# Output projection of a two-layer hybrid trunk: post-norm weight and residual on VectorE in place, and the next layer's first turns pinned behind tiles 3 and 5

## The chip, the cores and the metric

The kernel runs on one core of a Trainium2 chip. The metric is device time in microseconds (us) of one execution. Engines are named as in the profile: PE is TensorE's matmul queue (PEld its weight loads), DVE is VectorE, ACT is ScalarE, POOL is GpSimd, and SP is SyncE, which here only issues DMAs.

## The reference

Two layers, each over 1024 rows of 1024 features. What the change touches is the end of a layer and the start of the next one: the output product, the post-norm with its weight `post_g`, the residual, and the next layer's pre-norm.

```python
def rms_norm(x, g):
    xf = x.astype(jnp.float32)
    y = xf * lax.rsqrt(jnp.mean(xf * xf, axis=-1, keepdims=True) + EPS)
    return (y * g.astype(jnp.float32)).astype(x.dtype)

def hybrid_layer(x, positions, pre_g, w_in, ..., branch_g, w_out, post_g):
    h = rms_norm(x, pre_g)
    proj = h @ w_in
...
    y = jnp.concatenate([
        rms_norm(ya, branch_g[:LRU_WIDTH]),
        rms_norm(yb, branch_g[LRU_WIDTH:LRU_WIDTH + MLA_WIDTH]),
        rms_norm(yc, branch_g[LRU_WIDTH + MLA_WIDTH:]),
    ], axis=-1)
    return x + rms_norm(y @ w_out, post_g)
```

## The kernel before

All arithmetic is fp32; a product is made of three matmuls of split operands (`mm3`, L124 to L126). A layer ends with the output projection (loop from L1084), over eight tiles `t` of 128 rows.

For each tile, `project(t, 0, 5)` splits five of the eight k-slices of the branch outputs Y into high and low parts (ACT L356, POOL L357), runs 30 matmuls into one PSUM tile (pw_63) and moves the result to the SBUF tile `z` with the row scale `ra` (ACT L1001). `project(t, 5, 8)` does the same for the other three slices with 18 matmuls into pw_64, and DVE L1003 adds its result, scaled by `rb`, to `z`. So a tile is 48 matmuls, and its pw_63 must have been read by L1001 before the next tile's first part may write there. Tiles 0 and 1 have their first part made early, inside the attention stage.

Then the post-norm and the residual: POOL L1096 writes `zg = z * g` into a third buffer; `row_rsqrt` forms the row's factor `r` (a sum of squares on ACT L318, then two small POOL instructions, L132 and L133); DVE L1100 makes `z = zg * r + x` in one instruction; SP stores it (L1101). In layer 0 the next layer's pre-norm follows: the same ACT L318, POOL L132 and L133, and DVE L329, which writes the normalised tile into the buffer that held `x` (tiles 0 to 3) or into free halves of Y (tiles 4 to 7). After tiles 1 and 3, `turn_pair` transposes a pair of normalised tiles on PE (16 turns of 128x128, L340, into the four PSUM tiles pa_65 to pa_68) and splits them (ACT L346, DVE L347) into the next layer's left operand. From tile 4 on the next layer's first weights W are loaded (SP L366) and split (ACT L375; the low part on POOL or DVE, L376). The last tile is handled in column pieces of 512, 256 and 256.

Buffers `z`, `zg`, `x` and the loaded W come from one pool of seven tiles of 128x1024 (F_134 to F_140; F_140 holds the post-norm weight here); R tiles hold the split operands. Within an engine instructions run in a fixed order that a list scheduler chose when the program was built; `keep` (used by the change) pins a chain of instructions to the order in which the code is written. Whatever waits at the head of an engine's queue holds all that stands behind it.

Of the kernel before, what the change touches and what calls it, by code (L numbers as in the profile page):

```python
# [12 lines left out]
ALU = mybir.AluOpType  # L13
# [4 lines left out]
NT = T // 128  # L18
DEPTH = 2
# [68 lines left out]
def trunk_kernel(tc, A, out):  # L88
    nc = tc.nc
    keep = tc.keep_in_program_order  # L90
    V, S_, G, PE = nc.vector, nc.scalar, nc.gpsimd, nc.tensor
# [20 lines left out]
    def bank(kind):  # L112
        turn[kind] = (turn[kind] + 1) % len(banks[kind])
        return banks[kind][turn[kind]]
# [4 lines left out]
    def SM(n):  # L119
        ring_at[0] = (ring_at[0] + 1) % 48  # L120
        return ring[:, ring_at[0], 0:n]

    def mm3(ps, sh, sl, mh, ml, start, stop):
        PE.matmul(ps, lhsT=sh, rhs=mh, start=start, stop=False)  # L124
        PE.matmul(ps, lhsT=sh, rhs=ml, start=False, stop=False)  # L125
        PE.matmul(ps, lhsT=sl, rhs=mh, start=False, stop=stop)  # L126

    def rsqrt(ms, n, out=None):

        y = SM(n) if out is None else out  # L130
        x = SM(n)
        G.tensor_scalar(out=x, in0=ms, scalar1=EPS, scalar2=None, op0=ALU.add)  # L132
        G.tensor_tensor(out=y, in0=x, in1=mhalf[:, 0:n], op=ALU.pow)  # L133
        return y

    identr = cst.tile([128, 128], F32R, name="ident")
    ident = identr.bitcast(F32)
# [25 lines left out]
    FS = Slots(cst, NF, 1024, F32, "F")  # L163
# [10 lines left out]
    def load_x(src, t):  # L174
        x = FS.take((128, 2, 512))
        nc.sync.dma_start(out=x, in_=src[t * 128:(t + 1) * 128, :].rearrange("p (a b) -> p a b", b=512))
        return x
# [133 lines left out]
    def row_rsqrt(xs, cols=((0, 1024),), order=lambda i: i):  # L311

        n = len(xs) * len(cols)
        ms = SM(n)
        for i in range(n):
            q = HS.take((128, 512))
            c = slice(*cols[i // len(xs)])
            order(S_.activation(q.bitcast(BF16)[:, c], xs[i % len(xs)].rearrange("p a b -> p (a b)")[:, c],  # L318
                                AF.Square, scale=1.0 / 32, accum_out=ms[:, i:i + 1]))
            HS.give(q)  # L320
        if len(cols) > 1:
            V.scalar_tensor_tensor(out=ms[:, 0:1], in0=ms[:, 0:1], scalar=ms[:, 1:2], in1=ms[:, 2:3], op0=ALU.add,
                                   op1=ALU.add)
        return rsqrt(ms[:, 0:len(xs)], len(xs))

    def prenorm(xs, ns, order=lambda i: i, eng=None):
        r = row_rsqrt(xs, order=order)
        for i, (x, n) in enumerate(zip(xs, ns)):
            (eng or V).tensor_scalar(out=n, in0=x, scalar1=r[:, i:i + 1], scalar2=None, op0=ALU.mult)  # L329
        return ns  # L330

    def turn_pair(l, xn, hT, pair, slots):

        half, o = pair // 2, (pair % 2) * 256
        for kk in range(4):
            ps = bank("P1")
            pv = ps.rearrange("p (k t) -> p k t", k=2)
            for j in range(2):
                for i in range(2):
                    PE.transpose(pv[:, j, i * 128:(i + 1) * 128],  # L340
                                 xn[i][:, kk // 2, (2 * (kk % 2) + j) * 128:(2 * (kk % 2) + j + 1) * 128], ident)
            h, lo = hT[half][kk]
            for j in range(2):
                hs = h[:, j, o:o + 256]
                g = pg[:, l * 8 + 2 * kk + j:l * 8 + 2 * kk + j + 1]
                S_.activation(hs, pv[:, j], AF.Copy, scale=g)  # L346
                V.scalar_tensor_tensor(out=lo[:, j, o:o + 256], in0=pv[:, j], scalar=g, in1=hs.bitcast(F32),  # L347
                                       op0=ALU.mult, op1=ALU.subtract)
        for x in xn:
            slots.give(x)  # L350

    def new_hT():
        return [(RS.take((128, 2, 512)), RS.take((128, 2, 512))) for _ in range(4)]

    def split(src, h, lo, eng=None):
        S_.activation(h, src, AF.Copy)  # L356
        (eng or G).tensor_tensor(out=lo, in0=src, in1=h.bitcast(F32), op=ALU.subtract)  # L357
# [175 lines left out]
    xn = [load_x(A["x"][0], t) for t in range(2)]  # L533
    ws = {0: W(0, 0, 256, 4)}
    xn += [load_x(A["x"][0], t) for t in range(2, 4)]
    hT = [new_hT()]
    x4 = [load_x(A["x"][0], t) for t in range(4, NT)]
    ws[1] = W(0, 256, 256, 4, now=False)
    prow = load_params()
    prenorm(xn[:2], xn[:2])  # L540
    turn_pair(0, xn[:2], hT, 0, FS)
    prenorm(xn[2:], xn[2:])
    for p in range(2):
        prenorm(x4[2 * p:2 * p + 2], x4[2 * p:2 * p + 2], keep, G)
    turn_pair(0, xn[2:], hT, 1, FS)
    ws[1].split(keep)
    turn_params(prow)
    xn, xs = x4, FS

    for l in range(DEPTH):  # L550

        xc, last, gw = {}, [], []
# [31 lines left out]
        for p in range(2):  # L584
            turn_pair(l, xn[2 * p:2 * p + 2], hT, 2 + p, xs)
# [115 lines left out]
        for t in range(NT):  # L701
            if t % 4 == 0:
# [5 lines left out]
                                   op0=ALU.add, op1=ALU.mult)  # L708
# [52 lines left out]
        for t in range(NT):  # L761
            if t % 2 == 0:
# [8 lines left out]
                            in1=CK[:, t:t + 1].to_broadcast([128, 2, 16]), op=ALU.mult)  # L771
            V.scalar_tensor_tensor(out=r2[:, 1, 0:16], in0=kr[:, 16:32], scalar=-1.0, in1=SK[:, t], op0=ALU.mult,
                                   op1=ALU.mult)
            V.tensor_tensor(out=r2[:, 1, 16:32], in0=kr[:, 0:16], in1=SK[:, t], op=ALU.mult)
            V.tensor_tensor(out=ln[:, 192:256].rearrange("p (a b) -> p a b", a=2),
                            in0=r2[:, 0:1].to_broadcast([128, 2, 32]), in1=r2[:, 1:2].to_broadcast([128, 2, 32]),
                            op=ALU.add)
            r = rsqrt(ms, 2)
# [3 lines left out]
            if t % 4 == 3:  # L782
                half = t // 4
                hs = slice(half * 512, (half + 1) * 512)
                for b in range(3):
# [8 lines left out]
                    for r0, n, h, r1, lo in todo:  # L794
# [3 lines left out]
                                        op=ALU.subtract)  # L798
# [186 lines left out]
        def tile_cols(t):  # L985
            return ((0, 512), (512, 768), (768, 1024)) if t == NT - 1 else ((0, 1024),)

        def project(t, a, b, bufs=None):
            ts = slice(t * 128, (t + 1) * 128)
            yh, yl, z = bufs or (RS.take((128, 8, 128)), RS.take((128, 8, 128)), FS.take((128, 2, 512)))  # L990
            split(Y[:, a:b, ts], yh[:, a:b], yl[:, a:b], G)
            ps = bank("P2")
            zf = z.rearrange("p a b -> p (a b)")
            for c0, c1 in tile_cols(t):
                c = slice(c0, c1)
                for k in range(a, b):
                    for d in range(c0, c1, 512):
                        cs = slice(d, min(d + 512, c1))
                        mm3(ps[:, cs], yh[:, k], yl[:, k], wo[k][0][:, cs], wo[k][1][:, cs], k == a, k == b - 1)
                if a == 0:  # L1000
                    S_.activation(zf[:, c], ps[:, c], AF.Copy, scale=ra[:, t:t + 1])  # L1001
                else:
                    V.scalar_tensor_tensor(out=zf[:, c], in0=ps[:, c], scalar=rb[:, t:t + 1], in1=zf[:, c],  # L1003
                                           op0=ALU.mult, op1=ALU.add)
            return yh, yl, z
# [75 lines left out]
        if l + 1 < DEPTH:  # L1081
            hT = [new_hT()]
        xn = []
        for t in range(NT):  # L1084
            ts = slice(t * 128, (t + 1) * 128)
            xo = load_x(src, t)
            yh, yl, z = started.pop(t, None) or project(t, 0, 5)
            cols = tile_cols(t)
            project(t, 5, 8, (yh, yl, z))
            RS.give(yh)  # L1090
            RS.give(yl)
            zg = FS.take((128, 2, 512))
            zf, zgf, xf, gf = [v.rearrange("p a b -> p (a b)") for v in (z, zg, xo, gpost)]
            for c in cols:
                c = slice(*c)
                G.tensor_tensor(out=zgf[:, c], in0=zf[:, c], in1=gf[:, c], op=ALU.mult)  # L1096
            r = row_rsqrt([z], cols)
            for c in ((0, 512), (512, 1024)) if t == NT - 1 else cols:
                c = slice(*c)
                V.scalar_tensor_tensor(out=zf[:, c], in0=zgf[:, c], scalar=r, in1=xf[:, c], op0=ALU.mult, op1=ALU.add)  # L1100
                nc.sync.dma_start(out=(x1_dram if l == 0 else out[0])[ts, c], in_=zf[:, c])  # L1101
            FS.give(zg)
            if l + 1 < DEPTH:
                if t < 4:
                    xn += prenorm([z], [xo])
                    if t % 2:
                        turn_pair(l + 1, xn, hT, t // 2, FS)
                        xn = []
                else:
                    if t == 4:  # L1110
                        for y in yhalf:
                            YS.lend(y)
                        ws = {0: W(l + 1, 0, 256, 4)}
                        xs = YS
                    n = YS.take((128, 2, 512))
                    xn += prenorm([z], [n])
                    FS.give(xo)
            else:
                FS.give(xo)
            FS.give(z)  # L1120
# [26 lines left out]
```

## Time and profile before

| | before |
|---|---|
| time, median of 3 runs (lowest, highest) | 927.14 us (925.89, 928.77) |
| profiled execution, its own time | 928.23 us |
| its span in the trace | 926.5 us |
| mean granted PE clock, share of full | 0.991 |
| busy: PE, DVE, ACT, POOL | 879.8, 568.7, 520.1, 425.4 us |

The profiled execution is 1.09 us above the median. The output projection of layer 0 lies at about 385 to 475 us of the span, that of layer 1 at about 850 to 926 us. A duration is the time of one instruction; "idle before" is how long its engine had nothing to do until it, and the arrow names what ended that. PE instructions overlap, so for PE the distance from start to start is the pace. Line numbers of rows are those of the kernel before.

### The profile page before, as it was taken

The page shows a single profiled execution, that of the slowest core. Times are in us where ns is not written, and L with a number is a line of the kernel's source. Part 1 is how long each engine was busy: PE and PEld are TensorE (multiplying, and loading weights), DVE is VectorE, ACT ScalarE, POOL GpSimd, SP SyncE. Part 2 cuts the span into 40 slices and gives each one's busy share as a digit, 9 for nine tenths or more (in the row PEclk, how much of TensorE's full clock was granted, in tenths as well). Part 3 has the DMA queues.
Part 4 walks back from the last instruction along what each step waited for, and adds up shares of the span by engine and source line. Part 5 has one row for each costly group of instructions (what it writes and reads, how often), then busy time and mean ns, then how long its engine had stood idle before and what let it go on. Part 6 is the DMA issues. An engine that isn't in the chain of part 4 may idle for free. (4 is left out here: it accounts for less than half of the span.)

```text
span 926.5 us, 13666 instructions
## 1 busy us (share of the span) xinstructions
PE 879.8 (95%) x5078; PEld 778.1 (84%) x5078; DVE 568.7 (61%) x1078; ACT 520.1 (56%) x1032; POOL 425.4 (46%) x461
## 2 busy tenths in 40 slices
PE   4999997999999999989999999989989999999996
PEld 3998786998889889868887888889978999998786
DVE  4567955735689897454456488434554989853322
ACT  6447744554777778444544386354466877754312
POOL 4720056564045567384743000665530567655822
PEclk9999998999999999998999999999999999999999
DMA  7201365322000253022324022753110015221322
GB/s 274 55 25 49 110 226 178 123 100 59 14 1 4 89 182 115 23 91 87 118 93 122 1 80 86 288 201 131 49 23 0 1 47 193 81 69 46 126 102 91
DMA packets 45080, 86.93 MB, mean 94 GB/s; under 512 B 8825, under 2 KB 26837, under 8 KB 45013
## 3 DMA queue, kind: packets, MB, share of 16 engines
q1 hardware_dynamic: 35796, 52.50, 17.8%
q0 software_dynamic: 6912, 25.17, 7.7%
q10 hardware_dynamic: 2304, 8.39, 2.3%
q8 instruction: 40, 0.66, 0.3%
q14 instruction: 28, 0.22, 0.1%
HBM read 60.88 MB, written 25.17 MB: 93 GB/s over the span
## 5 line engine op out<-in xcount | busy, mean ns | idle before, releaser
L124 PE MATMUL pw<-R,R 128*128 128x512 f32 (+1 forms) x704 | 259.7, 370 | 5.1 <-DVE R L357 2.1
L126 PE MATMUL pw<-R,R 128*128 128x512 f32 (+1 forms) x704 | 253.0, 360 | 0.7 <-POOL R L376 0.7
L125 PE MATMUL pw<-R,R 128*128 128x512 f32 (+1 forms) x704 | 253.3, 360 | 0.0
L124 PE MATMUL pa<-R,R 128*128 128x512 f32 (+3 forms) x540 | 187.3, 349 | 11.6 <-DVE F L707 6.6
L125 PE MATMUL pa<-R,R 128*128 128x512 f32 (+3 forms) x540 | 186.1, 345 | 0.0
L126 PE MATMUL pa<-R,R 128*128 128x512 f32 (+3 forms) x540 | 185.2, 345 | 0.0
L124 PEld LDWEIGHTS pw<-R,R 128*128 128x128 f32 x704 | 135.0, 192 | 25.7 <-ACT F L937 2.7
L126 PEld LDWEIGHTS pw<-R,R 128*128 128x128 f32 x704 | 134.9, 192 | 19.1 <-POOL R L376 1.1
L125 PEld LDWEIGHTS pw<-R,R 128*128 128x128 f32 x704 | 135.2, 192 | 17.2
L124 PEld LDWEIGHTS pa<-R,R 128*128 128x128 f32 x540 | 102.0, 189 | 22.5 <-DVE F L707 7.1
L939 POOL TENSOR_SCALAR F<-F,ring 128x128 f32<-128x128 f32 (+3 forms) x96 | 72.7, 762 | 89.5 <-DVE ring L938 87.9
L126 PEld LDWEIGHTS pa<-R,R 128*128 128x128 f32 x540 | 101.8, 189 | 9.9
L125 PEld LDWEIGHTS pa<-R,R 128*128 128x128 f32 x540 | 102.2, 189 | 8.6
L357 DVE TENSOR_TENSOR R<-pa,R 128x512 fp32r<-128x512 f32 (+1 forms) x120 | 73.9, 630 | 16.7 <-ACT R L356 15.7
L937 ACT ACTIVATE F<-pw,ring 128x128 f32<-128x128 f32 (+3 forms) x96 | 71.1, 743 | 21.1 <-DVE ring L935 18.4
L935 DVE TENSOR_REDUCE ring<-pw 128x1 f32<-128x128 f32 (+3 forms) x96 | 71.6, 749 | 11.3 <-PE pw L928 10.7
L356 ACT ACTIVATE R<-pa 128x512 fp32r<-128x512 f32 (+1 forms) x120 | 63.8, 554 | 19.2 <-PE pa L959 17.6
L376 POOL TENSOR_TENSOR R<-F,R 128x1024 fp32r<-128x1024 f32 (+1 forms) x24 | 54.2, 2265 | 42.2 <-ACT R L375 42.2
L968 PE MATMUL pa<-R,R 128*128 128x256 f32 x480 | 72.1, 288 | 0.5 <-DVE R L357 0.5
L968 PEld LDWEIGHTS pa<-R,R 128*128 128x128 f32 x480 | 63.4, 189 | 3.6 <-DVE R L357 1.1
L959 PE MATMUL pa<-ident,F 128*128 128x128 f32 x432 | 63.6, 273 | 0.7 <-DVE H L892 0.4
L357 POOL TENSOR_TENSOR R<-Y,R 128x640 fp32r<-128x640 f32 (+2 forms) x34 | 48.9, 1455 | 27.4 <-ACT R L356 10.2
(300 smaller groups left out, 1360.8 us busy)
## 6 DMA issues: line engine op xcount, KB each, us to landing
F<-in_w_in SPq DMA_DIRECT2D x24, 512.0 KB, 4.7
F<-in_x SPq DMA_DIRECT2D x13, 512.0 KB, 4.7
F<-in_w_out SPq DMA_DIRECT2D x9, 512.0 KB, 3.5
F<-x SPq DMA_DIRECT2D x8, 512.0 KB, 4.5
Y<-in_w_out SPq DMA_DIRECT2D x7, 512.0 KB, 4.4
x<-F SPq DMA_DIRECT2D x7, 512.0 KB
out_y<-F SPq DMA_DIRECT2D x7, 512.0 KB
Y<-in_w_in SPq DMA_DIRECT2D x6, 512.0 KB, 3.6
```

Of the source, the lines that this page charges most:

```text
L124: PE.matmul(ps, lhsT=sh, rhs=mh, start=start, stop=False)
L125: PE.matmul(ps, lhsT=sh, rhs=ml, start=False, stop=False)
L126: PE.matmul(ps, lhsT=sl, rhs=mh, start=False, stop=stop)
L356: S_.activation(h, src, AF.Copy)
L357: (eng or G).tensor_tensor(out=lo, in0=src, in1=h.bitcast(F32), op=ALU.subtract)
L376: self.eng.tensor_tensor(out=lo, in0=st, in1=h.bitcast(F32), op=ALU.subtract)
L935: V.tensor_reduce(out=mx, in_=sv, axis=AX.XY, op=ALU.max, negate=True)
L937: S_.activation(p[:, 0:n].rearrange("p (a b) -> p a b", a=sv.shape[1]), sv, AF.Exp, bias=mx, accum_out=sm)
L939: G.tensor_scalar(out=p[:, 0:n], in0=p[:, 0:n], scalar1=rs, scalar2=1.0, op0=ALU.mult, op1=ALU.mult)
L959: PE.transpose(pv[:, c, i * 128:(i + 1) * 128], p[i][:, b * 128:(b + 1) * 128], ident)
L968: PE.matmul(o, lhsT=sv, rhs=pt[:, part, c * 256:(c + 1) * 256], start=(b == 0 and part == 0), stop=(b == nb - 1 and part == 1))
```

## The change

For tiles 0 to 6 of both layers, POOL L1096 and its buffer `zg` go. DVE does two instructions in place of one, both on `z` itself: `z = z * r * g`, then `z = z + x`. The last tile keeps the old form. `turn_pair` no longer follows tiles 1 and 3: it stands between the two parts of `project` for tile 3 (pair of tiles 0 and 1) and tile 5 (pair of tiles 2 and 3), and its transposes are pinned with `keep`.

```diff
--- before.py
+++ after.py
@@ -329,7 +329,7 @@
             (eng or V).tensor_scalar(out=n, in0=x, scalar1=r[:, i:i + 1], scalar2=None, op0=ALU.mult)
         return ns
 
-    def turn_pair(l, xn, hT, pair, slots):
+    def turn_pair(l, xn, hT, pair, slots, order=lambda i: i):
 
         half, o = pair // 2, (pair % 2) * 256
         for kk in range(4):
@@ -337,8 +337,9 @@
             pv = ps.rearrange("p (k t) -> p k t", k=2)
             for j in range(2):
                 for i in range(2):
-                    PE.transpose(pv[:, j, i * 128:(i + 1) * 128],
-                                 xn[i][:, kk // 2, (2 * (kk % 2) + j) * 128:(2 * (kk % 2) + j + 1) * 128], ident)
+                    order(PE.transpose(pv[:, j, i * 128:(i + 1) * 128],
+                                       xn[i][:, kk // 2, (2 * (kk % 2) + j) * 128:(2 * (kk % 2) + j + 1) * 128],
+                                       ident))
             h, lo = hT[half][kk]
             for j in range(2):
                 hs = h[:, j, o:o + 256]
@@ -1086,26 +1087,35 @@
             xo = load_x(src, t)
             yh, yl, z = started.pop(t, None) or project(t, 0, 5)
             cols = tile_cols(t)
+            if l + 1 < DEPTH and t in (3, 5):
+                turn_pair(l + 1, xn[:2], hT, t // 4, FS, keep)
+                xn = xn[2:]
             project(t, 5, 8, (yh, yl, z))
             RS.give(yh)
             RS.give(yl)
-            zg = FS.take((128, 2, 512))
+            last = t == NT - 1
+            zg = FS.take((128, 2, 512)) if last else z
             zf, zgf, xf, gf = [v.rearrange("p a b -> p (a b)") for v in (z, zg, xo, gpost)]
-            for c in cols:
+            if last:
+                for c in cols:
+                    c = slice(*c)
+                    G.tensor_tensor(out=zgf[:, c], in0=zf[:, c], in1=gf[:, c], op=ALU.mult)
+            r = row_rsqrt([z], cols)
+            for c in ((0, 512), (512, 1024)) if last else cols:
                 c = slice(*c)
-                G.tensor_tensor(out=zgf[:, c], in0=zf[:, c], in1=gf[:, c], op=ALU.mult)
-            r = row_rsqrt([z], cols)
-            for c in ((0, 512), (512, 1024)) if t == NT - 1 else cols:
-                c = slice(*c)
-                V.scalar_tensor_tensor(out=zf[:, c], in0=zgf[:, c], scalar=r, in1=xf[:, c], op0=ALU.mult, op1=ALU.add)
+                if last:
+                    V.scalar_tensor_tensor(out=zf[:, c], in0=zgf[:, c], scalar=r, in1=xf[:, c], op0=ALU.mult,
+                                           op1=ALU.add)
+                else:
+                    V.scalar_tensor_tensor(out=zf[:, c], in0=zf[:, c], scalar=r, in1=gf[:, c], op0=ALU.mult,
+                                           op1=ALU.mult)
+                    V.tensor_tensor(out=zf[:, c], in0=zf[:, c], in1=xf[:, c], op=ALU.add)
                 nc.sync.dma_start(out=(x1_dram if l == 0 else out[0])[ts, c], in_=zf[:, c])
-            FS.give(zg)
+            if last:
+                FS.give(zg)
             if l + 1 < DEPTH:
                 if t < 4:
                     xn += prenorm([z], [xo])
-                    if t % 2:
-                        turn_pair(l + 1, xn, hT, t // 2, FS)
-                        xn = []
                 else:
                     if t == 4:
                         for y in yhalf:
```

In the listings below the names are those of the tiles: pw and pa are PSUM, F and R SBUF; the changed kernel's lines are a little shifted (L1002 for L1001, L1004 for L1003, L347 and L348 for L346 and L347).

PE, layer 0, around the first turns. Before, between the second part of tile 2 (pw_64 with R_107, R_112) and the first of tile 3 (pw_63 with R_117, R_118):

```order
L125 MATMUL pw_64<-R_131,R_107 128x512
L126 MATMUL pw_64<-R_128,R_112 128x512
L340 MATMUL pa_67<-ident,F_139 128x128
L340 MATMUL pa_68<-ident,F_139 128x128
L340 MATMUL pa_65<-ident,F_139 128x128
L340 MATMUL pa_66<-ident,F_139 128x128
L124 MATMUL pw_63<-R_123,R_117 128x512
L125 MATMUL pw_63<-R_101,R_117 128x512
```

After, at the start of tile 3's second part (pw_64 with R_117, R_118):

```order
L126 MATMUL pw_63<-R_105,R_118 128x512
L124 MATMUL pw_64<-R_125,R_117 128x512
L340 MATMUL pa_67<-ident,F_139 128x128
L125 MATMUL pw_64<-R_126,R_117 128x512
L126 MATMUL pw_64<-R_125,R_118 128x512
```

Of the 16 turns of the first pair, four stood at the border of tiles 2 and 3; now one stands 31 matmuls later and the other 15 a further 17 matmuls later, behind tile 3's last one. The second pair's 16 turns stand together between the two parts of tile 5.

ACT, layer 0, tiles 5 to 7 (F_137 is tile 5's z in both; tile 6's is F_134 before and F_139 after; H tiles take the squares). Before:

```order
L1001 ACTIVATE F_137<-pw_63,ra 128x1024
L375 ACTIVATE R_130<-F_139 128x1024
L318 ACTIVATE H_143,ring<-F_137 128x1024
L1001 ACTIVATE F_134<-pw_63,ra 128x1024
L318 ACTIVATE H_142,ring<-F_137 128x1024
L318 ACTIVATE H_141,ring<-F_134 128x1024
```

After:

```order
L347 ACTIVATE R_132<-pa_65,pg 128x256
L347 ACTIVATE R_110<-pa_66,pg 128x256
L318 ACTIVATE H_143,ring<-F_137 128x1024
L318 ACTIVATE H_142,ring<-F_137 128x1024
L1002 ACTIVATE F_139<-pw_63,ra 128x1024
L318 ACTIVATE H_141,ring<-F_139 128x1024
L1002 ACTIVATE F_138<-pw_63,ra 128x512
```

The evacuation of tile 6's first part (L1001, now L1002) stood ahead of tile 5's pre-norm square (the second L318 on F_137) and now stands behind it.

DVE, layer 0, tile 3 (z is F_135 before, F_137 after). Before:

```order
L347 SCALAR_TENSOR_TENSOR R_129<-pa_68,pg,R_109 128x256
L347 SCALAR_TENSOR_TENSOR R_116<-pa_65,pg,R_132 128x256
L347 SCALAR_TENSOR_TENSOR R_106<-pa_66,pg,R_110 128x256
L1003 SCALAR_TENSOR_TENSOR F_135<-pw_64,rb,F_135 128x1024
L1100 SCALAR_TENSOR_TENSOR F_135<-F_137,ring,F_139 128x1024
L329 TENSOR_SCALAR F_139<-F_135,ring 128x1024
L1003 SCALAR_TENSOR_TENSOR F_138<-pw_64,rb,F_138 128x1024
```

After:

```order
L1004 SCALAR_TENSOR_TENSOR F_137<-pw_64,rb,F_137 128x1024
L348 SCALAR_TENSOR_TENSOR R_108<-pa_67,pg,R_121 128x256
L348 SCALAR_TENSOR_TENSOR R_129<-pa_68,pg,R_109 128x256
L348 SCALAR_TENSOR_TENSOR R_116<-pa_65,pg,R_132 128x256
L348 SCALAR_TENSOR_TENSOR R_106<-pa_66,pg,R_110 128x256
L1110 SCALAR_TENSOR_TENSOR F_137<-F_137,ring,F_140 128x1024
L348 SCALAR_TENSOR_TENSOR R_108<-pa_67,pg,R_121 128x256
L348 SCALAR_TENSOR_TENSOR R_129<-pa_68,pg,R_109 128x256
L348 SCALAR_TENSOR_TENSOR R_116<-pa_65,pg,R_132 128x256
L348 SCALAR_TENSOR_TENSOR R_106<-pa_66,pg,R_110 128x256
L1112 TENSOR_TENSOR F_137<-F_137,F_138 128x1024
L329 TENSOR_SCALAR F_138<-F_137,ring 128x1024
```

The first pair's eight low parts (L347, now L348) came ahead of tile 3's L1003 before; now they lie between its L1003 and its two new instructions.

The first two W loads move too: they go to F_136 and F_137 (F_136 and F_139 before) and are issued in tile 3 (behind the first pair's turns, which free F_136) and behind the store of tile 3; on ACT their splits (L375) now stand ahead of the pre-norm squares of tiles 3 and 4, and on POOL (L376) ahead of the splits of tiles 5 and 6.

## Rows read from the trace of the kernel before

**Rows 1.** The page's busy time, share and count of each engine.
```profile
PE 879.8 (95%) x5078; PEld 778.1 (84%) x5078; DVE 568.7 (61%) x1078; ACT 520.1 (56%) x1032; POOL 425.4 (46%) x461
```

**Rows 2.** Waits of PE, 400 to 510 us: total, times, longest.
```profile
PE pa L340 <- DVE F L329: 3.9, 1, 3.9
...
PE pa L340 <- DVE Y L329: 0.5, 1, 0.5
```

**Rows 3.** Waits of PE, 820 us to the end.
```profile
PE pw L124 <- ACT F L1001: 0.7, 1, 0.7
```

**Rows 4.** Timeline of PE, tiles 2 and 3: start, duration, instruction, idle before.
```profile
408.95 0.40 PE L126 MATMUL pw<-R,R 128*128 128x512 f32 x1
...
411.70 0.39 PE L126 MATMUL pw<-R,R 128*128 128x512 f32 x1
415.98 1.11 PE L340 MATMUL pa<-ident,F 128*128 128x128 f32 x4 [3.89 <-DVE F L329]
417.17 0.79 PE L124 MATMUL pw<-R,R 128*128 128x512 f32 x1
...
422.34 0.39 PE L124 MATMUL pw<-R,R 128*128 128x512 f32 x1
...
424.18 1.47 PE L340 MATMUL pa<-ident,F 128*128 128x128 f32 x12
```

**Rows 5.** Stretches: length, busy (PE, PEld, DVE, ACT, POOL), granted PE clock, DMA share, GB/s.
```profile
416.00:420.00 4.00, 3.92 (x11) 2.94 (x12) 1.95 (x2) 2.27 (x3) 1.86 (x3) 0.50 0.13 52
...
424.00:428.00 4.00, 4.00 (x25) 3.47 (x24) 1.95 (x5) 3.29 (x9) 0.52 (x2) 1.00 0.33 90
```

**Rows 6.** Timeline of POOL, tiles 0 and 1.
```profile
402.63 2.58 POOL L1096 TENSOR_TENSOR F<-F,F 128x1024 f32<-128x1024 f32 x1
405.17 3.38 POOL L357 TENSOR_TENSOR R<-Y,R 128x384 fp32r<-128x384 f32 x3
...
408.97 0.59 POOL L133 TENSOR_TENSOR ring<-ring,mhalf 128x1 f32<-128x1 f32 x1
```

**Rows 7.** Timeline of DVE, tiles 0 and 1.
```profile
409.59 1.28 DVE L1100 SCALAR_TENSOR_TENSOR F<-F,ring,F 128x1024 f32<-128x1024 f32 x1 [1.09 <-POOL ring L133]
...
415.17 0.75 DVE L329 TENSOR_SCALAR F<-F,ring 128x1024 f32<-128x1024 f32 x1 [0.78 <-POOL ring L133]
```

**Rows 8.** Groups by line and shape, whole span: busy us, mean ns, idle before.
```profile
L376 POOL TENSOR_TENSOR R<-F,R 128x1024 fp32r<-128x1024 f32 x16 | 39.9, 2503 | 38.0 <-ACT R L375 38.0
L1096 POOL TENSOR_TENSOR F<-F,F 128x1024 f32<-128x1024 f32 x14 | 33.7, 2409 | 41.2 <-DVE F L1003 41.0
L318 ACT ACTIVATE H<-F 128x1024 bf16<-128x1024 f32 x27 | 28.6, 1058 | 44.4 <-DVE F L1003 23.4 <-DVE F L1100 14.2 <-DMA F<-in_x 5.0
L347 DVE SCALAR_TENSOR_TENSOR R<-pa,pg,R 128x256 fp32r<-128x256 f32 x64 | 27.6, 476 | 17.7 <-ACT R L346 17.0 <-PE pw L125 0.3
...
L1003 DVE SCALAR_TENSOR_TENSOR F<-pw,rb,F 128x1024 f32<-128x1024 f32 x14 | 17.9, 1280 | 19.8 <-PE pw L126 19.8
...
L1001 ACT ACTIVATE F<-pw,ra 128x1024 f32<-128x1024 f32 x14 | 15.7, 1118 | 30.9 <-issue 17.4 <-PE pw L126 13.0 <-ACT H L318 0.4
...
L485 DVE TENSOR_TENSOR Y<-Y 128x1024 f32<-128x1024 f32 x3 | 3.7, 1223 | 0.8 <-ACT Y L481 0.8
```

**Rows 9.** Timeline of POOL, layer 1, tile 0.
```profile
855.91 12.63 POOL L357 TENSOR_TENSOR R<-Y,R 128x384 fp32r<-128x384 f32 x9
```

**Rows 10.** Timeline of DVE, layer 1, tile 0.
```profile
855.98 2.02 DVE L1100 SCALAR_TENSOR_TENSOR F<-F,ring,F 128x1024 f32<-128x1024 f32 x1 [4.00 <-POOL ring L133]
```

**Rows 11.** A stretch in layer 1 (columns as in rows 5).
```profile
680.00:684.00 4.00, 1.38 (x11) 0.90 (x9) 3.59 (x10) 2.29 (x6) 3.47 (x3) 1.00 0.03 9
```

**Rows 12.** Timeline of SP's queue, layer 0, tile 4: the first two W loads.
```profile
448.07 0.93 SPq L366 DMA_DIRECT2D F<-in_w_in  x2
```

**Rows 13.** Timeline of ACT there: the first W split.
```profile
451.78 1.06 ACT L375 ACTIVATE R<-F 128x1024 fp32r<-128x1024 f32 x1 [0.39 <-DMA F<-in_w_in]
```

**Rows 14.** The page's DMA issues: count, KB each, us to landing.
```profile
F<-in_w_in SPq DMA_DIRECT2D x24, 512.0 KB, 4.7
```

## The prediction

> **What bounds the kernel now.** I read the busy times first: PE works through 95% of the span [rows 1], so an edit on DVE and POOL can only pay where PE waits. So the waits of PE come next, in the two stretches that the change touches. In layer 0 one stands out, 3.9 us for DVE's L329 ahead of the first turns, and a later one of 0.5 [rows 2]; in layer 1 there is one of 0.7 us for L1001 [rows 3].
>
> The timeline shows what the long one costs [rows 4]. The last matmul ahead of it starts at 411.70. From 408.95 to there twelve matmuls take 2.75 us, 0.229 each, so PE could have gone on at 411.93. The next matmul starts at 417.17, 5.24 us later; four turns belong in between, 0.12 each by the twelve at 424.18, so 4.75 us are lost. And PE came back at half speed: the granted clock reads 0.50 in 416 to 420, the lower of its two levels (1.2 against 2.4 GHz), and 1.00 again from 424 [rows 5]. The twelve matmuls from 417.17 to 422.34 take 5.17 us where twelve took 2.75: 2.42 us more. This place costs 4.75 + 2.42 = 7.2 us, nearly twice what the wait's row says.
>
> Why did the turns wait? L329 of tile 0 ran at 415.17 [rows 7], at the end of a chain through POOL. There a multiply by the weight (2.58 us) and three splits stood ahead of the small operations that make tile 0's r, which came at 409.56 [rows 6]; only then could L1100 run, at 409.59.
>
> **The change part by part.** POOL loses 14 multiplies of 2.41 us, 33.7 us [rows 8]; POOL isn't the bound, so this gives nothing by itself. DVE gets a second instruction for each of 14 tiles. L1100 alone took 1.28 us [rows 7], and the nearest row for the added sum is L485 of the same size, 1.22 us [rows 8]: 17 us on an engine that is busy 568.7 of 926.5. Off the path that is nothing; its price is 1.22 us in each chain from L1003 to the next L1001, below.
>
> *The first turns.* Without the two multiplies tile 0's r comes 2.5 us sooner or more. PE now does not ask for tile 0 before 31 matmuls past 411.93, 31 x 0.229 = 7.1 us, thus at 419.0, against 415.98 when L329 had delivered it late. That wait of 4.75 us goes, and with it the 2.42 us of half clock. Next to be late is tile 1, asked for 17 matmuls later, at 422.9. Laid out in the listed order, DVE does tile 1's sum and tile 2's two instructions ahead of tile 1's L329, and POOL's small operations wait beside them; I get 420.5 to 423.9, so a wait of 0 to 1.0 us, and take 0.6.
>
> *The evacuation behind the squares.* L1001 of the next tile now stands behind a tile's pre-norm square on ACT. From L1003 that chain is 1.28 (L1003) + 1.06 (L318) + 1.0 (r: from the splits' end at 408.55 to 409.56 [rows 6]) + 1.28 + 1.22 (the two new instructions) + 1.06 (L318 again) + 1.12 (L1001) = 8.0 us [rows 6 to 8]. A tile of 48 matmuls lasts 48 x 0.229 = 11.0 us, so 3.0 us are left, and it is those that the moved turns use up.
> Tile 3: PE needs tile 4's L1001 after 15 turns and 48 matmuls, 12.8 us. To the 8.0 come 0 to 2.3 us in which L1003 stands behind L329 of tile 2 (0.75 [rows 7], and by my estimate up to 1.5 until its r is there), four L347 of 0.48 between the two new instructions, 1.9, and up to 2.5 if W's split on POOL (L376 [rows 8]) has started just then and holds the second one up, as below. The sum is 8.0 to 14.7 (each of these can overlap the rest), a wait of 0 to 1.9 us at tile 5's first matmul; I take 1.3, since the listed orders put all three there, the split in part.
> Tile 5: eight L347 stand ahead of its L1003, 8 x 0.48 = 3.8 us. They may begin when the turns are done, 18 matmuls (4.1 us) ahead of L1003's turn, if ACT is free; but ACT does L1001 of tile 5 first, itself behind tile 4's square. They end 3 to 5 us late, 0 to 2.0 past the room, at tile 7's first matmul. Before, L1001 stood ahead of that square. I take 1.6.
> Then the W loads. The first was issued at 448.07 [rows 12] and split from 451.78 [rows 13]; now it is asked for some 20 us sooner. Its landing is covered as long as it takes under some 7 us from its issue, since ACT then waits for tile 3's sum anyway; the page's median is 4.7 [rows 14]. The second one's landing can hold tile 5's L1001: 0 to 2.5 us; I take 0.
> The wait of 0.5 us for tile 4's L329 at the next layer's start [rows 2] follows tile 7 and may double: 0.4.
>
> *The shared port.* In layer 1 an L1100 that started at 855.98, just behind POOL's splits, took 2.02 us instead of 1.28 [rows 9, 10], so a DVE instruction with both inputs in SBUF stands still for a POOL instruction that came first. The Trainium skill states this as a rule (SBUF — State Buffer, section "Who interferes with whom"): such an instruction and a GpSimd one that reads SBUF exclude each other, the first one for its whole length. The trace agrees, with the 0.74 us above. By that rule the change doubles what can be locked out, 28 instructions in place of 14, but also takes 14 long holders away. Were there no such lock, the 1.3 at tile 3 would be nothing, and the sum 1.3 us lower.
>
> *Layer 1.* No turns here. Tile 0's L1100 no longer waits behind a multiply, a z buffer is free sooner, and with zg gone nobody wants a third one; the 0.74 us goes. The last tile is as before, and the tiles ahead of it have 11 us each for a shorter chain.
>
> The sum: saved 4.75 + 2.42 + 0.74 = 7.9; new 0.6 + 1.3 + 1.6 + 0.4 = 3.9; net -4.0. The profiled execution was 928.23, so 924.2; the median of the runs lies 1.09 lower, so **923.1**.
>
> **The rivals.** *No new waits.* All four come out at their lower ends. For it: most engines have idle time here and the scheduler's order is only a list; against: three separate items each have to vanish. Net -7.9: 919.2.
> *The new waits take it all back.* All at their upper ends: 1.0 + 1.9 + 2.0 + 0.5 and 2.5 for the second W, 7.9: net 0, 927.1; with most of them, 925 to 927. For it: every one is the same pattern, ACT holding PSUM's release behind a chain that got longer.
> *Slower: the second W load.* ACT's split of it stands ahead of tile 4's square and tile 5's L1001. If it lands 10 us after its issue instead of 4.7 (it meets two stores and two loads of x on the queue), 5.3 us are added there: a wait longer than the 3.89 that halved the clock, so 2.4 more, and the other items stay. Net -7.9 + 5.3 + 2.4 + 3.9 = +3.7: 930.8. It decides from a wait of about 4 us: in layer 1 two shorter ones, the first 1.33, left 1.38 us of PE work in 4 us, and the clock stayed at 1.00 [rows 11].
> *The change doesn't do what it says*: excluded, as far as the listings show the turns behind tile 3 and tile 5.
>
> **How the numbers follow.** A measurement of this kernel tells about 0.3% from no change, 2.8 us: faster is under 924.4, slower over 929.9. Forecast with new waits of 2 to 5 us: 0.50, nearly all faster. No new waits: 0.17, faster. Taken back: 0.25, most within 0.3%. Slower: 0.08. Faster 0.65, same 0.27, slower 0.08. The range goes from just under the first rival to the third, 918.8 to 927.3, and leaves out the slow one and the far ends.
>
> **What would show it.** Right: no wait for L329 ahead of the turns, granted clock 1.00 at 416 to 424, a POOL without multiplies, no wait for L1001 in layer 1, and new waits of 0.5 to 2 us on L1001 at tiles 5 and 7 of layer 0. Wrong: any wait of 3 us or more with the clock at 0.50 behind it; L1001 of tile 5 held by the second W; the two new DVE instructions well over 1.3 us each in many tiles; or the gain in layer 0 taken back at the next layer's first products, which wait for loads or splits that have not become earlier.

## The result

The changed kernel takes 919.1 us (median of 5 runs, 918.13 to 922.87) against 927.14: a ratio of 0.9917, with a 95% interval of 0.9894 to 0.9940. Twice more, beside other kernels, it measured 920.37 us (0.9933, 0.9914 to 0.9952) and 919.57 us (0.9932, 0.9910 to 0.9954), so the gain is 6 to 8 us. That is inside the stated range, close to the rival without new waits (919.2), and about twice the forecast of 4. The sections below show that the reason given for the largest term was only half of it.

The page of the changed kernel gives the busy time of each engine:

```profile
PE 877.1 (96%) x5078; PEld 777.1 (85%) x5078; DVE 583.9 (64%) x1092; ACT 520.3 (57%) x1032; POOL 395.1 (43%) x447
```

Beside [rows 1] DVE has 14 instructions and 15.2 us more, POOL 14 instructions and 30.3 us less. Now PE's waits in the stretch of [rows 2], 400 to 510 us (engine, what waited, for what: total, times, longest):

```profile
PE pw L124 <- ACT F L1002: 1.9, 1, 1.9
PE pa L124 <- DVE R L348: 1.6, 1, 1.6
```

The wait of 3.9 us ahead of the first turns is gone, as is the 0.5 at the next layer's start (0.7 in two later profiles of this kernel); the one of 0.7 in layer 1 [rows 3] is gone too. The 1.6 (for L347, now L348) was there before. Where the clock was halved before [rows 5] it is not now (columns as in rows 5):

```profile
410.00:420.00 10.00, 10.00 (x46) 8.23 (x45) 8.52 (x7) 4.54 (x8) 7.26 (x9) 1.00 0.42 157
420.00:430.00 10.00, 10.00 (x53) 8.51 (x52) 8.66 (x13) 6.68 (x14) 3.82 (x6) 1.00 0.34 107
```

New is one wait, at tile 7's first matmul. PE's timeline there (start, duration, instruction, idle before), then stretches (columns as in rows 5):

```profile
456.77 0.60 PE L340 MATMUL pa<-ident,Y 128*128 128x128 f32 x4
459.32 0.50 PE L124 MATMUL pw<-R,R 128*128 128x512 f32 x1 [1.95 <-ACT F L1002]
...
459.91 0.63 PE L126 MATMUL pw<-R,R 128*128 128x512 f32 x1
460.34 0.63 PE L124 MATMUL pw<-R,R 128*128 128x512 f32 x1
```
```profile
460.00:462.00 2.00, 2.00 (x6) 1.57 (x5) 1.20 (x2) 0.77 (x1) 0.00 (x0) 0.50 0.00 0
...
464.00:466.00 2.00, 2.00 (x15) 1.78 (x14) 1.97 (x3) 1.34 (x3) 0.00 (x0) 1.00 0.00 0
```

The wait is 1.95 us, and behind it matmuls start 0.43 us apart instead of 0.23, with the granted clock at 0.50.

Where the time went can be read by matching the two traces' matmuls one to one (both PE programs do the same 5078 instructions; hardly any but the turns change places) and taking how far the changed kernel is ahead. By the two timelines:

| stretch | gained (us) |
|---|---|
| start to layer 0's attention | 2.3 |
| layer 0, tiles 2 to 6 | 7.35 |
| layer 0, tile 7's first part | -3.8 |
| start of layer 1 | 1.3 |
| middle of layer 1 | 1.0 |
| layer 1, tile 1 | 1.0 |
| sum | 9.1 |

The first line isn't the change's: up to there every engine runs the same instructions in the same order in both kernels. PE waits there for L707, 6.4 us in this execution of the kernel before and 3.7 in this one of the changed kernel; in the other profiled executions below it is 3.8 to 7.5. Nor can the middle of layer 1 be told from chance: that stretch (600 to 665 us of the kernel before) took 64.97 us there, and 64.03, 63.51 and 64.61 us in three executions of the changed kernel. In the two later profiles of the changed kernel tiles 2 to 6 and layer 1's tile 1 gain the same as here, tile 7 loses 2.2 us, and the start of layer 1 gains 0.1 and 0.4. That makes about 6.3 and 6.6 us, which agrees with the 6 to 8 between medians.

### The profile page after: what moved, and what is told of

It reads as the page before. It is cut to its first block, busy times and chain, and to the rows that moved or that the text cites. A ratio compares the mean times of both kernels' runs of the same rounds, so it can differ in the third digit from the quotient of the medians.

```text
span 917.3 us, 13660 instructions
## 1 busy us (share of the span) xinstructions
PE 877.1 (96%) x5078; PEld 777.1 (85%) x5078; DVE 583.9 (64%) x1092; ACT 520.3 (57%) x1032; POOL 395.1 (43%) x447
## 5 line engine op out<-in xcount | busy, mean ns | idle before, releaser
L358 DVE TENSOR_TENSOR R<-pa,R 128x512 fp32r<-128x512 f32 (+1 forms) x120 | 73.9, 629 | 16.5 <-ACT R L357 15.6
L377 POOL TENSOR_TENSOR R<-F,R 128x1024 fp32r<-128x1024 f32 (+1 forms) x24 | 55.2, 2307 | 45.8 <-ACT R L376 45.8
L318 ACT ACTIVATE H<-F 128x1024 bf16<-128x1024 f32 (+2 forms) x33 | 31.4, 953 | 55.6 <-DVE F L1004 33.4
```

What stands on the lines that cost most here:

```text
L377: self.eng.tensor_tensor(out=lo, in0=st, in1=h.bitcast(F32), op=ALU.subtract)
```

## The experiments

Ratios are to the kernel before, measured beside it; times are medians. Lines are numbered as in the changed kernel, give or take two. The scheduler makes a new order on every engine for almost every edit, so these kernels differ in more than the lines shown. Only the kernel with the evacuation first is the changed kernel's program with one ACT instruction moved.

**One part alone: in place.** The turns go back to where they stood in the code.

```diff
-            if l + 1 < DEPTH and t in (3, 5):
-                turn_pair(l + 1, xn[:2], hT, t // 4, FS, keep)
-                xn = xn[2:]
...
                     xn += prenorm([z], [xo])
+                    if t % 2:
+                        turn_pair(l + 1, xn, hT, t // 2, FS)
+                        xn = []
```

> Only the two in-place DVE instructions; the turns stand in the code where they stood before (after tiles 1 and 3, not pinned). In the listed order the scheduler itself now puts the first pair's turns 31 and 48 matmuls later, nearly where the change pins them; the second pair's stand 12 of 16 inside tile 5's first part. Theory (what counts is that PE asks for tile 0 late enough and that its r comes early; the pin itself adds nothing): no wait of 3.9 us ahead of the first turns, the granted clock 1.00 there, 917 to 921 us. Rival (the pinned place is what pays): a wait of 2 us or more ahead of turns stays and the time is 923 to 927.

Measured: 928.43 us, ratio 1.0016 (1.0002 to 1.0031). Neither expectation held: nothing waits ahead of the turns, yet the time is that of the kernel before. PE's timeline, then ACT's:

```profile
422.08 1.47 PE L340 MATMUL pa<-ident,F 128*128 128x128 f32 x12
430.06 0.79 PE L124 MATMUL pw<-R,R 128*128 128x512 f32 x1 [6.50 <-ACT F L1002]
```
```profile
427.95 1.06 ACT L376 ACTIVATE R<-F 128x1024 fp32r<-128x1024 f32 x1 [3.98 <-DMA F<-in_w_in]
428.91 1.10 ACT L1002 ACTIVATE F<-pw,ra 128x1024 f32<-128x1024 f32 x1
```

The wait moved by a tile. Tile 4's first matmul needs tile 3's evacuation (L1002), and that stands in ACT's queue behind the split of W (L376), which sat 4 us waiting for its load.

**The other part alone: turns moved and pinned**, with POOL's multiply and the third buffer kept.

```diff
+            if l + 1 < DEPTH and t in (3, 5):
+                turn_pair(l + 1, xn[:2], hT, t // 4, FS, keep)
+                xn = xn[2:]
             project(t, 5, 8, (yh, yl, z))
...
                     xn += prenorm([z], [xo])
-                    if t % 2:
-                        turn_pair(l + 1, xn, hT, t // 2, FS)
-                        xn = []
```

> Only the turns moved and pinned; POOL's multiply and the third buffer stay. Theory: tile 0's pre-norm came at 415.2 to 415.9 in the kernel before and is asked for at about 419 now, so the 4.75 us of wait and 2.42 us of half clock go also without the DVE part, unless the longer chain through POOL makes tile 1 or the next evacuations late: 919 to 923 us, with the 0.7 us wait in layer 1 still there. Rival (the multiply on POOL is what makes things late): waits of 2 us or more at tiles 3 to 7, 924 us or more.

Measured: 937.66 us, ratio 1.0110 (1.0089 to 1.0131), slower than the kernel before. The rival's waits and time came, and the theory, which was the forecast's largest step, fell. Whether POOL's multiply is the reason, as the rival has it, the next run tests. PE, then DVE, then ACT:

```profile
415.97 0.80 PE L124 MATMUL pw<-R,R 128*128 128x512 f32 x1 [5.13 <-ACT F L1002]
...
460.85 0.80 PE L124 MATMUL pw<-R,R 128*128 128x512 f32 x1 [4.56 <-ACT F L1002]
```
```profile
413.96 0.75 DVE L329 TENSOR_SCALAR F<-F,ring 128x1024 f32<-128x1024 f32 x1 [0.78 <-POOL ring L133]
```
```profile
414.80 1.11 ACT L1002 ACTIVATE F<-pw,ra 128x1024 f32<-128x1024 f32 x1 [0.43 <-ACT H L318]
...
459.69 1.11 ACT L1002 ACTIVATE F<-pw,ra 128x1024 f32<-128x1024 f32 x1 [2.45 <-POOL R L377]
```

The turns no longer stand at the border of tiles 2 and 3, but PE waits there as long as before, now for tile 2's evacuation. This one starts 0.1 us behind the end of tile 0's L329 (414.71). In the kernel before the same can be read once one looks for it:

```profile
416.01 1.11 ACT L1001 ACTIVATE F<-pw,ra 128x1024 f32<-128x1024 f32 x1 [0.44 <-ACT H L318]
```

It started 0.09 us after tile 0's L329 of 415.17 [rows 7] had ended and itself ended at 417.12, right ahead of PE's first matmul at 417.17 [rows 4]. In the program of the kernel before the two read and write the same buffer:

```
L329 TENSOR_SCALAR F_139<-F_138,ring 128x1024
L1001 ACTIVATE F_138<-pw_63,ra 128x1024
```

With three buffers a tile, tile 2's z is tile 0's, and it comes free when tile 0's L329 has read it. So two things waited for the same L329: the turns, and behind them, unseen, the evacuation. In ACT's queue the evacuation also stands behind the pre-norm squares of tiles 0 and 1 (the `ACT H L318` of its row), so with this order the buffer by itself holds it for the last 0.44 us. In the kernels with two buffers a tile the scheduler lists it ahead of both squares, as the next run shows. The second wait, of 4.56 us, is the same pattern at tile 6: L1002 writes into a buffer that W holds until POOL has split it (L377).

**POOL in two buffers.** The weight is multiplied in place on POOL, and DVE does one instruction; everything else in the code is as in the changed kernel.

```diff
-                    V.scalar_tensor_tensor(out=zf[:, c], in0=zf[:, c], scalar=r, in1=gf[:, c], op0=ALU.mult,
-                                           op1=ALU.mult)
-                    V.tensor_tensor(out=zf[:, c], in0=zf[:, c], in1=xf[:, c], op=ALU.add)
+                    G.tensor_tensor(out=zf[:, c], in0=zf[:, c], in1=gf[:, c], op=ALU.mult)
+                    V.scalar_tensor_tensor(out=zf[:, c], in0=zf[:, c], scalar=r, in1=xf[:, c], op0=ALU.mult,
+                                           op1=ALU.add)
```

> The changed kernel with the weight multiplied in place on POOL, after the square, and one DVE instruction per tile as before: two buffers a tile and the pinned turns, but the work on the engine where it was. Theory (what pays is the third buffer given back, since tile 2's first part then has a z at once and its evacuation no longer stands behind two pre-norm squares; the engine matters little): within 3 us of the changed kernel, 919 to 923, no wait of 3 us or more at tile 3. Rival (DVE instead of POOL is what pays): 925 us or more, the wait of about 5 us at tile 3 is back.

Measured: 926.7 us, ratio 0.9996 (0.9975 to 1.0017). Half of each: tile 2's evacuation follows PE's last matmul at once, as it does in the changed kernel, and the wait of 5 us at tile 3's first matmul didn't come back, so it was the buffer. ACT in the changed kernel, then in this one:

```profile
405.29 1.11 ACT L1002 ACTIVATE F<-pw,ra 128x1024 f32<-128x1024 f32 x1 [3.90 <-PE pw L126]
```
```profile
408.35 1.11 ACT L1002 ACTIVATE F<-pw,ra 128x1024 f32<-128x1024 f32 x1 [3.93 <-PE pw L126]
```

But on POOL the multiply now stands between the two small instructions that make r, and it takes 2.4 us, twice as long as DVE's sum; waits came elsewhere. PE's waits at the turns behind tile 3 (for tile 1's L329) and at tile 6, and the granted clock in both (columns as in rows 5):

```profile
426.76 1.85 PE L340 MATMUL pa<-ident,F 128*128 128x128 f32 x15 [2.85 <-DVE F L329]
...
454.80 0.50 PE L124 MATMUL pw<-R,R 128*128 128x512 f32 x1 [2.61 <-ACT F L1002]
```
```profile
427.00:429.00 2.00, 2.00 (x18) 1.91 (x17) 1.53 (x2) 2.00 (x5) 1.41 (x2) 1.00 0.00 0
...
456.00:458.00 2.00, 2.00 (x10) 1.64 (x10) 2.00 (x5) 0.57 (x2) 0.00 (x0) 1.00 0.39 158
```

A third new wait, 2.7 us, stands at the start of layer 1. Buffer and engine both count.

**The residual sum on POOL** instead of DVE:

```diff
-                    V.tensor_tensor(out=zf[:, c], in0=zf[:, c], in1=xf[:, c], op=ALU.add)
+                    G.tensor_tensor(out=zf[:, c], in0=zf[:, c], in1=xf[:, c], op=ALU.add)
```

> The changed kernel with the residual sum on POOL instead of DVE for tiles 0 to 6 of both layers, still in place in two buffers. Theory (the chain from L1003 to the next evacuation sets the waits): each chain is 1.2 us longer (2.4 for 1.2), the wait at tile 7 grows from 1.95 to some 3 us, tile 1's pre-norm is late by 0 to 2 us, 920 to 924 us. Rival (two DVE instructions that lock each other out with POOL cost more than a longer chain): same as the changed kernel or faster, 917 to 919.

Measured: 921.52 us, ratio 0.9950 (0.9931 to 0.9968), some 1 to 3 us slower than the changed kernel, at the edge of what can be told. The chain theory's price is right, and tile 1 is late as it said, but the wait that it put at tile 7 came elsewhere: PE's waits from 408 to 486 us are 3.0 in two pieces for L1002 (1.43 at tile 5, 1.58 at a later column piece of the last tile, none at tile 7's first matmul) and 1.1 for tile 1's L329, which shows how thin its margin is.

```profile
PE pw L124 <- ACT F L1002: 3.0, 2, 1.6
PE pa L340 <- DVE F L329: 1.1, 1, 1.1
```

**The evacuation first.** In the changed kernel tile 6's L1002 is put ahead of tile 5's pre-norm square on ACT, and nothing else moves.

```diff
             yh, yl, z = started.pop(t, None) or project(t, 0, 5)
+            while late:
+                late.pop()()
...
-                    S_.activation(zf[:, c], ps[:, c], AF.Copy, scale=ra[:, t:t + 1])
+                    pin = keep if l == 0 and t == 6 else (lambda i: i)
+                    pin(S_.activation(zf[:, c], ps[:, c], AF.Copy, scale=ra[:, t:t + 1]))
...
+                    if t == 5:
+                        xn += [n]
+                        late.append(lambda z=z, xo=xo, n=n: (prenorm([z], [n], keep), FS.give(xo), FS.give(z)))
+                        continue
```

> The changed kernel with one ACT instruction moved: in layer 0 the evacuation of tile 6's first part (L1001 of the kernel before) is put ahead of tile 5's pre-norm square, nothing else moves. Theory (the wait of 1.95 us at tile 7's first matmul comes from that queueing, and the half clock behind it, twelve matmuls' worth of 1.5 us, comes from the wait): both go, 3.4 us in all, 915 to 917 us. Rival (tile 5's pre-norm, now later, makes the next layer's first products wait): gain under 1 us, with a new wait at the first turns of the next layer.

Measured: 922.56 us, ratio 0.9950 (0.9935 to 0.9965). The rival holds in kind. The wait at tile 7's first matmul is gone, and PE is 3.1 us further there than in the first profile of the changed kernel, but two new ones follow. One, at 467.70, is for L1005 (L1003 of the kernel before) of the last tile's first column piece; the other, at 470.63, is for tile 6's L329, ahead of the next layer's turns:

```profile
PE pa L340 <- DVE Y L329: 1.6, 1, 1.6
PE pw L124 <- DVE F L1005: 1.1, 1, 1.1
```

By the matched matmuls the 3.1 us are lost again: at the next layer's turns 0.1 is left. What is late is DVE's chain, and the order on ACT only chooses who sees it.

**W later.** The changed kernel with the next layer's first W loads at tile 5 instead of 4.

```diff
                     if t == 4:
                         for y in yhalf:
                             YS.lend(y)
-                        ws = {0: W(l + 1, 0, 256, 4)}
                         xs = YS
+                    if t == 5:
+                        ws = {0: W(l + 1, 0, 256, 4)}
```

> The changed kernel with the first W loads of the next layer issued at tile 5 instead of tile 4. Theory (tile 7's wait of 1.95 us and its half clock of 1.5 us begin with W: tile 5's z takes the buffer that W's second part holds until POOL has split it, so tile 5's evacuation, the eight splits behind it and tile 5's L1003 are some 5 us late): tile 7's wait is under 0.5 us, no half clock there, 2 to 3.5 us less than the changed kernel, with W still ready for the next layer. Rival (the eight splits of the second pair alone make tile 5's L1003 late): tile 7's wait stays at 1 us or more; or W comes too late and the next layer's first products wait 2 us or more.

> The changed kernel with the first W loads at tile 5, once more, to tell 2 us. Theory (the wait of 2 us at tile 7, with or without 1.5 us of half clock, is worth its size): 1.5 to 3.5 us under the changed kernel of this call. Rival (what tile 7 gains is lost at the next layer's start, where a wait of 1.2 us for another instruction had appeared): within 1 us of it.

Measured: 918.42 us (0.9919, 0.9895 to 0.9943) beside 920.37 for the changed kernel, and 917.43 (0.9929, 0.9902 to 0.9957) beside 919.57. Both times 2 us less, the low end of what the theories said, though the intervals overlap. ACT and DVE around tile 5's end, first in the changed kernel:

```profile
444.44 1.12 ACT L1002 ACTIVATE F<-pw,ra 128x1024 f32<-128x1024 f32 x1 [1.04 <-POOL R L377]
445.45 1.92 ACT L347 ACTIVATE R<-pa,pg 128x256 fp32r<-128x256 f32 x5
```
```profile
451.09 1.27 DVE L1004 SCALAR_TENSOR_TENSOR F<-pw,rb,F 128x1024 f32<-128x1024 f32 x1
```

and with W later:

```profile
441.95 1.10 ACT L1002 ACTIVATE F<-pw,ra 128x1024 f32<-128x1024 f32 x1
442.95 1.56 ACT L347 ACTIVATE R<-pa,pg 128x256 fp32r<-128x256 f32 x4
```
```profile
448.18 1.27 DVE L1004 SCALAR_TENSOR_TENSOR F<-pw,rb,F 128x1024 f32<-128x1024 f32 x1
```

Tile 5's evacuation waited for POOL's split of W, since its z is W's buffer; then the eight splits and L1003 (L1004 here) were late. Without it all run 2.5 to 3 us sooner, PE's wait at tile 7 is gone, and one of 1.2 us for another instruction (L441) stands at layer 1's start. But the 2 us are not tile 7's alone. By the matched stretches this kernel loses 1.4 us ahead of tile 2, where the order is new too (PE waits 0.63 us there for a split on POOL, L358), gains 2.3 at tile 7 against the two later profiles of the changed kernel, and gains another 1.4 to 1.9 at layer 1's start. Its medians are the lowest found.

**In place alone, W later.** Both edits above, turns unpinned where they stood in the code.

> The in-place part alone (turns where they stood in the code) with the first W loads at tile 5 instead of tile 4. In the run of the in-place part alone PE waited 6.5 us at tile 4 for an evacuation that stood behind ACT's split of W, which waited 4 us for its load, and 1.9 us of half clock followed. Theory (that split in the queue is what takes the in-place part's gain): the wait falls to 1 to 2.5 us (tile 3's z is the buffer that the first pair's last turn frees), the half clock goes, 919 to 923 us. Rival (the unpinned turns hold tile 3's z, W or no W): a wait of 4 us or more there, 926 or more.

> The in-place part with later W loads and turns where they stood in the code, once more, since its profile before was taken in a disturbed execution. Theory (the pinned place of the turns is not needed once W is out of the way): the time of the changed kernel, 918 to 922 us, and a wait at tile 4 of at most 2.5 us. Rival (the time before was a lucky one): 924 us or more.

Measured: 919.91 us (0.9934, 0.9910 to 0.9958) and 919.69 (0.9937, 0.9922 to 0.9953), the time of the changed kernel. In the second run's profile PE has no wait at all from 408 to 486 us; tile 3's evacuation runs at 424.81 instead of 428.91, with no load to wait for:

```profile
424.81 1.13 ACT L1002 ACTIVATE F<-pw,ra 128x1024 f32<-128x1024 f32 x1
```

The 1.4 us lost ahead of tile 2 are in these times too. So with W later the pinned turns are not needed for the gain; in the changed kernel they are one way to keep W's split from getting ahead of an evacuation.

**Turns alone, W later.**

> The moved and pinned turns alone (POOL's multiply and the third buffer stay) with the first W loads at tile 5 instead of tile 4. Theory (two separate things made the turns alone slower: at tile 3 PE waits for tile 2's evacuation, which needs the z of tile 0 and so the same L329 for which the turns waited, 5.1 us; at tile 6 it waits 4.6 us for an evacuation into a buffer that W holds): the first wait stays at 4.5 to 5.5 us at about 416, the second falls under 1.5, 927 to 932 us. Rival (one cause, the moved turns themselves, lies behind both): both waits stay, 935 us or more.

Measured: 930.35 us, ratio 1.0042 (1.0028 to 1.0057): the theory's range. The wait of 4.6 us at tile 6 is gone (one of 1.2 stands at tile 7, one of 2.4 for L441 at layer 1's start). That at tile 3 stays, though at 2.86 us instead of 4.5 or more: here POOL's order has the first two multiplies ahead of the splits, and tile 0's L329 comes 1.5 us sooner than with the turns alone. Little is gained by that, since by the matched stretches PE has lost 2.2 us more ahead of 408 us (1.43 of it waiting for a split on POOL, L358). DVE and ACT there, where this time the profile names the releaser itself:

```profile
412.46 0.75 DVE L329 TENSOR_SCALAR F<-F,ring 128x1024 f32<-128x1024 f32 x1 [0.76 <-POOL ring L133]
```
```profile
413.39 1.11 ACT L1002 ACTIVATE F<-pw,ra 128x1024 f32<-128x1024 f32 x1 [0.50 <-DVE F L329]
```

**The changed kernel again**, twice:

> The changed kernel once more, beside the next three on the same chip. Both theories: 918 to 922 us; how much of its own runs' spread (918.13 to 922.87) is there again says how finely the others can be compared.

> The changed kernel a third time, beside the one with later W loads. Both theories: 918 to 922 us; in the profile the wait of about 2 us at tile 7, with half clock behind it in some executions and not in others.

Measured: 920.37 us (918.49 to 922.99, 10 runs) and 919.57 us (917.94 to 921.86, 6 runs). Both profiles have the wait at tile 7, and neither the half clock behind it. PE and the stretch, from the first of them:

```profile
460.65 0.50 PE L124 MATMUL pw<-R,R 128*128 128x512 f32 x1 [1.99 <-ACT F L1002]
460.99 0.39 PE L125 MATMUL pw<-R,R 128*128 128x512 f32 x1
```
```profile
462.00:464.00 2.00, 2.00 (x11) 1.64 (x10) 0.54 (x1) 1.15 (x2) 0.19 (x1) 1.00 0.00 0
```

## Why the prediction was right, and where it was wrong

*What bounds the kernel.* Right: the wait at the first turns and the half clock behind it were priced at 4.75 + 2.42 = 7.2 us, and tiles 2 to 6 gained 7.35.

*The first turns.* The size was right and the reason half wrong. The step said that the wait goes because PE asks for tile 0's turns later. The turns alone leave it at 5.13 us, since tile 2's evacuation needs tile 0's z and thus the same L329. The trace of before had this, in ACT's row 0.05 us ahead of PE's matmul, but the prediction took the named releaser for the only one. What ends this wait is the third buffer given back, which the prediction counted only within layer 1's 0.74 us; with the buffer free, the evacuation runs at 405.29 in the changed kernel. That the term came out at its size is to that extent luck: the same change happened to give the buffer back. Giving it back on POOL also ends the wait, but the longer chain costs as much elsewhere (926.7 us). And in-place alone gains nothing until W's split is out of ACT's way. That neither half pays alone was in none of the rivals.

*The new waits*, 3.9 us in the sum, are where the number went off. Tile 1's turns: 0.6 expected, none came, with L329 done at 420.3 and the turns starting at 420.70; moving the sum to POOL showed 1.1. Tile 5's first matmul: 1.3 expected, none came; W's split did start 0.2 us behind tile 3's sum, and held nobody up. Tile 7: 1.6 expected, 1.95 came in the row, some 2.2 us by the matched matmuls, for the reason given (the eight splits ahead of L1003, then L1001 behind the square), and in the first profile 1.6 more for the half clock behind it, which the sum left out. The splits were late because tile 5's evacuation was held by the second W, a sign of being wrong that the prediction had named. It was held not by W's landing, which the prediction took at 0, but by its split on POOL: the 1.04 us idle in the row at 444.44. The next layer's start: 0.4 lost expected, 1.3 gained in this profile, about nothing in the two later ones, where a wait of 0.7 stands there. Layer 1: 0.74 expected, 1.04 gained.

*The shared port.* The groups of the two new instructions (columns as in rows 8), then DVE at tile 0 of layer 1:

```profile
L1110 DVE SCALAR_TENSOR_TENSOR F<-F,ring,F 128x1024 f32<-128x1024 f32 x14 | 19.3, 1381 | 25.7 <-POOL ring L133 25.6
L1112 DVE TENSOR_TENSOR F<-F,F 128x1024 f32<-128x1024 f32 x14 | 17.8, 1273 | 0.4
```
```profile
843.37 2.64 DVE L1110 SCALAR_TENSOR_TENSOR F<-F,ring,F 128x1024 f32<-128x1024 f32 x1
846.04 1.92 DVE L1112 TENSOR_TENSOR F<-F,F 128x1024 f32<-128x1024 f32 x1
```

They took 1.38 and 1.27 us in the mean where the prediction took 1.28 and 1.22, but no instruction took the mean: 13 of each 14 took 1.28 and 1.22, and the two shown stood 1.36 + 0.70 = 2.1 us longer, the first just behind a split on POOL that began at 843.36. The rule that the Trainium skill states (SBUF — State Buffer, "Who interferes with whom") is that a VectorE instruction with two inputs in SBUF and a GpSimd one that reads SBUF exclude each other. This place agrees with it. No row shows that the 2.1 us cost PE anything. In layer 0, where the 1.3 us at tile 3 hung on such a lock, none of the new instructions was longer. What took longer there was L329: 1.5 to 2.1 us in tiles 1 to 4 and 1.6 in tile 6, where the prediction took 0.75 (before, 2.1 in tile 2, 2.8 in tile 4 and 1.8 in tile 6).

*The clock.* The slow rival's "decides from a wait of about 4 us" was wrong: the clock was halved behind shorter waits too, as the last section shows.

## What to carry to other kernels

When a wait has one named releaser, look for what else came free at the same moment: the instruction that starts right behind the same event on another engine is the next wait, and moving the first consumer away gained nothing here. In a kernel with few buffers ask of each evacuation whose buffer it writes, and what stands ahead of it in its engine's queue; here a third buffer per tile and a load's split were each worth 2 to 7 us, on engines that were busy about half the time. Moving the evacuation past a square gained 3 us where it stood and lost them again within 10 us. Change one of two coupled things and the time may rise, so test the parts alone and together before judging either.

## What the hardware showed that was not expected

The granted clock after a short wait differs from execution to execution of the same program. In the changed kernel the wait of 1.95 us at tile 7 was followed by 0.50 in one profiled execution (1.6 us lost) and waits of 1.99 and 1.96 by 1.00 in two others, while 2.85 and 2.61 us in the kernel with POOL's multiply in place left it at 1.00 and 2.86 us in the one with the turns alone and W later halved it. In layer 1 all kernels have the same two waits of 1.33 and 1.54 us, one behind the other. The matmul behind the second took 0.69 to 0.80 us, and the granted clock fell, in 5 of the 13 profiled executions told of here; it took 0.50 us in the other 8. PE's row there in the changed kernel, then in the one with the evacuation first, with a stretch behind it:

```profile
676.19 0.50 PE L124 MATMUL pa<-R,R 128*128 128x512 f32 x1 [1.54 <-DVE Y L414]
```
```profile
676.95 0.79 PE L124 MATMUL pa<-R,R 128*128 128x512 f32 x1 [1.54 <-DVE Y L414]
...
678.00:680.00 2.00, 2.00 (x6) 1.61 (x5) 0.75 (x2) 0.37 (x1) 0.00 (x0) 0.50 0.01 4
```

That place cost that execution 2.7 us. So for the waits of 1.5 to 2.9 us seen here the length alone does not decide it, and what else does stays open. Among the three profiled executions of the changed kernel the half clock at tile 7 makes 1.6 us of difference, the first 200 us (with the wait for L707, 3.7 to 7.5 us in identical code) 2.1, and the middle of layer 1 1.1. Runs of that kernel differ by 4 to 5 us; that these places make up most of it is likely but not shown. Two profiled executions should therefore be compared stretch by stretch and not by their spans.
